# Four adaLN gates: column sums by VectorE and a trip through DRAM instead of an accumulated tile summed by TensorE

## The chip, the core and the metric

The kernel runs on one NeuronCore of a Trainium2 chip, in one launch. The metric is the device time of one execution in microseconds. Weights and activations lie in DRAM at the start; the output goes back to DRAM. The engines named below are TensorE (PE; its weight loads are PEld), VectorE (DVE), ScalarE (ACT), GpSimd (POOL) and SyncE (SP), which here only issues DMAs.

## The reference, cut to what matters

```python
def reference(x, c, ada_w, ada_b, na_w_qkv, na_rpb, na_w_o, fn_w_o, ...):
    cs = jax.nn.silu(c)
    for i in range(DEPTH):                               # DEPTH = 2, D_MODEL = 1024, SEQ = 512
        mod = jnp.einsum('bd,de->be', cs, ada_w[i]) + ada_b[i]
        sh1, sc1, g1, sh2, sc2, g2 = jnp.split(mod[:, None, :], 6, axis=-1)
        u = x * (1.0 + sc1) + sh1
        y = neighborhood_attention(u, ...) if i % 2 == 0 else fourier_mix(u, ...)
        x = layer_norm(ALPHA * x + (1.0 + g1) * y, ln1_g[i], ln1_b[i])
        u = x * (1.0 + sc2) + sh2
        y = conv_ffn(u, ...)                             # D_FF = 2816
        x = layer_norm(ALPHA * x + (1.0 + g2) * y, ln2_g[i], ln2_b[i])
    return x
```

Everything is float32. The four gates `g1`, `g2` of the two layers are vectors of 1024, each the product of the vector `cs` with a 1024x1024 block of `ada_w`, plus a bias. `1 + g` multiplies a sub-layer's output along the channel axis.

## The kernel before, in words

Each float32 matmul is done as three products of values split into a high and a low part (`mm3`), 128 rows by up to 512 columns each. Weights come in tiles of 512 KB into four `raw` buffers; ScalarE writes the high part (line 228), VectorE the low part (line 229). TensorE then works through these stages: the first q, k and v products; neighbourhood attention over eight pairs of heads; the output product `wo`; the first FFN's `up` (22 tiles `f`) and `dn` products; the Fourier mixer; the second FFN.

The conditioning weights, 12 blocks of 1024x1024, come in pieces `ada_l_v_k` through the same four `raw` buffers between the other weights, so that their loads and VectorE's work on them lie beside the matmuls. Blocks that are needed as a column per partition (shifts and scales) lie transposed in DRAM, and VectorE multiplies each piece with `cs_row` and sums it into one column (`weigh_rows`, line 128). The four gates, v = 2 and v = 5 of each layer, are needed as a row on all partitions, since channels lie along the free axis there. For them VectorE accumulates `acc += piece * cs[k]` over eight pieces (lines 151 and 153). `gate_row` then loads the bias row to all partitions (line 176), splits `acc` into a high and a low part in two halves (lines 166 and 167), sums it over the partitions by four products with a matrix of ones into two PSUM banks, and adds 1 and the bias row (line 185). This happens at pair i = 0 of the attention for the first gate, at f = 8 of the first `up`, f = 1 of the first `dn` and f = 14 of the second `up` for the others.

What sets the order: a tile scheduler places the instructions of each engine by its own estimate of times and by the buffers that are free; every engine, SyncE's DMA queue among them, then runs its list in that order, and a waiting instruction holds those behind it. Parts of the program are kept in written order on some engines (the first products, and the attention's pairs from i = 1). Buffers are shared by tags: four `raw`, two `bx` (slices of the position bias, for one head each, from which GpSimd builds the tiles `bm`, lines 514 to 520), six PSUM banks `bank` and two `aux`, thirty `big` tiles of 4 KB per partition.

The stretch around the first gate goes as follows. TensorE makes the value products of the second half of the heads (`v`, four banks), transposes the probabilities of heads 0 and 1 (`pt`), multiplies the scores of the next pair (`s`), the values (`av`), and then the q and k of pair 2 (`qk`). There are six banks. `v` holds four, the first head's `pt` the other two; the second head's `pt` takes the banks of the first two `v` once VectorE has moved these out, and `av` takes those of the second head's `pt`, once VectorE has written their low parts `ptl`. VectorE can do that when ScalarE has written the high parts `pth`.

Of the kernel before, what the change touches and what calls it, by code (L numbers as in the profile page):

```python
# [10 lines left out]
F32 = mybir.dt.float32  # L11
F32R = mybir.dt.float32r
AF = mybir.ActivationFunctionType
ALU = mybir.AluOpType

P = 128
# [38 lines left out]
def tile_hybrid_encoder(ctx: ExitStack, tc: tile.TileContext, xT, x, cols_d, rows_d, ada0, ada_w, wqk0, wqk, wv,  # L55
# [24 lines left out]
    def f32(ap):  # L80
        return ap.bitcast(F32)
# [11 lines left out]
    nc.sync.dma_start(out=cols, in_=cols_d)  # L93
    ident = const.tile([P, P], F32, name="ident")
    make_identity(nc, ident)
    ones_r = const.tile([P, P], F32R, name="ones_r")
    G.memset(f32(ones_r), 1.0)
    mhalf = const.tile([P, 1], F32, name="mhalf")
    G.memset(mhalf, -0.5)

# [22 lines left out]
            A.copy(out=cs_row[:, h * 512 : (h + 1) * 512], in_=b[h])  # L123


    def weigh_rows(raw, c, col, start):

        return V.tensor_tensor_reduce(out=raw, in0=raw, in1=cs_row[:, c], op0=ALU.mult, op1=ALU.add, scale=1.0,  # L128
                                      scalar=start, accum_out=col)

    def ada_columns(l, v, result):

        for k in range(KT):
            raw = wraw.tile([P, D], F32, tag="raw", name=f"ada_{l}_{v}_{k}")
            nc.sync.dma_start(out=raw, in_=ada_w[ADA[(l, v)], k])
            if k == 0:
                col = const.tile([P, KT], F32, name=f"col_{l}_{v}")
            weigh_rows(raw, slice(0, D), col[:, k : k + 1], adab(l, v)[:, k : k + 1])
            if k == KT - 1:
                result[(l, v)] = col  # L140
            yield

    def ada_accumulate(l, v, result):

        acc = None
        for k in range(KT):
            raw = wraw.tile([P, D], F32, tag="raw", name=f"ada_{l}_{v}_{k}")
            nc.sync.dma_start(out=raw, in_=ada_w[ADA[(l, v)], k])
            if k == 0:
                acc = bigt([P, D], F32, f"acc_{l}_{v}")  # L150
                V.tensor_scalar(out=acc, in0=raw, scalar1=cs[:, 0:1], scalar2=None, op0=ALU.mult)
            else:
                V.scalar_tensor_tensor(out=acc, in0=raw, scalar=cs[:, k : k + 1], in1=acc, op0=ALU.mult,
                                       op1=ALU.add)
            if k == KT - 1:
                result[(l, v)] = acc
            yield

    def ada_row_sums(acc, name):

        res = []
        for h in range(2):
            a = acc[:, h * 512 : (h + 1) * 512]
            hi = tmp.tile([P, 512], F32R, tag="t", name=f"{name}_hi{h}")
            lo = tmp.tile([P, 512], F32R, tag="t", name=f"{name}_lo{h}")
            A.copy(out=hi, in_=a)
            V.tensor_tensor(out=lo, in0=a, in1=f32(hi), op=ALU.subtract)
            b = bank(f"{name}_{h}", aux=True)
            mm(b, ones_r, hi, True, False)
            mm(b, ones_r, lo, False, True)  # L170
            res.append(b)
        return res

    def bcast_row(r, name):
        t = bigt([P, D], F32, name)
        nc.sync.dma_start(out=t, in_=rows_d[r : r + 1, :].to_broadcast([P, D]))
        return t

    def gate_row(accs, l, v, name):

        row = bcast_row(ROW_GATE + 2 * l + (0 if v == 2 else 1), f"{name}_row")
        bs = ada_row_sums(accs[(l, v)], name)
        for h in range(2):
            r = row[:, h * 512 : (h + 1) * 512]
            V.scalar_tensor_tensor(out=r, in0=bs[h], scalar=1.0, in1=r, op0=ALU.add, op1=ALU.add)
        return row

    def modulation(sh, sc, ln, name):

# [176 lines left out]
        return raws  # L366

    done = {}
    ada01 = const.tile([P, KT], F32, name="ada01")
    V.tensor_scalar(out=ada01, in0=adab(0, 1), scalar1=1.0, scalar2=None, op0=ALU.add)  # L370

    def cond(k):

        for b, start in enumerate((adab(0, 0), ada01)):
            o = mod0[:, (1 - b) * KT + k : (1 - b) * KT + k + 1]
            start = start[:, k : k + 1]
            if k == 0:
                half = sml.tile([P, 1], F32, tag="t0", name="half")
                weigh_rows(raws[k][b][:, 0:512], slice(0, 512), half, start)
                done["mod"] = weigh_rows(raws[k][b][:, 512:D], slice(512, D), o, half)  # L380
            else:
                done["mod"] = weigh_rows(raws[k][b], slice(0, D), o, start)
# [235 lines left out]

    def ada_iter():
        for l, v in ADA:  # L620
            yield from (ada_accumulate if v in (2, 5) else ada_columns)(l, v, accs)

    ada = ada_iter()

# [19 lines left out]
    for i in range(PAIRS - 1):  # L644
# [6 lines left out]
            qbank, kbank = proj_qk(i + 1)  # L651
            QK[i + 1] = evict_q(i + 1, qbank), evict_k(i + 1, kbank)
        if i == 0:
            gates[(0, 2)] = gate_row(accs, 0, 2, "g1_0")
        transpose_probs(i)
        if i + 2 == PAIRS:
            W.emit(iwo[3])
# [157 lines left out]
    def steps_up0(f):  # L815
        if 2 < f < 19:
            ada_step(2)
        if f == 8:
            gates[(0, 5)] = gate_row(accs, 0, 5, "g2_0")
        if f == FT - 1:  # L820
            W.emit(idn[0][0] + 1)
        if f == 16:
# [21 lines left out]
    def steps_dn0(f):  # L844
        if f < 8:
            ada_step(2)
        if f == 1:
            gates[(1, 2)] = gate_row(accs, 1, 2, "g1_1")
        if f == 8:
            fst["m3"] = modulation(accs[(1, 3)], accs[(1, 4)], (1, 0), "ffn1")  # L850
        if f == 8:
# [111 lines left out]
    def steps_up1(f):  # L963
        if f > 2:
            ada_step(1)
        if f == 14:
            gates[(1, 5)] = gate_row(accs, 1, 5, "g2_1")
        if f == FT - 1:
            W.emit(idn[1][0] + 1)

# [26 lines left out]
def _layouts(inputs):  # L997
# [30 lines left out]

    def piece(l, v):
        w = f["ada_w"][l][:, v * D : (v + 1) * D]  # L1030
        return (w if v in (2, 5) else w.T).reshape(KT, P, D)

    r["ada0"] = np.ascontiguousarray(np.stack([piece(0, 0), piece(0, 1)], axis=2))
    r["ada_w"] = np.ascontiguousarray(np.stack([piece(l, v) for l, v in ADA]))
# [59 lines left out]
```

## Time and profile before

| What | us |
| --- | --- |
| median of three runs | 1049.3 |
| lowest and highest run | 1049.18, 1050.73 |
| the profiled execution | 1050.14 |
| its span | 1048.1 |
| TensorE busy in the span | 1029.5 (98%) |
| VectorE, ScalarE, GpSimd busy | 759.5, 425.2, 102.6 |

The profiled execution lies 0.84 us above the median, and 2.0 us of it lie outside the span. A TensorE row of 128x512 is busy for 0.37 to 0.40 us, but the next one starts after 0.23 us: the rows overlap. So the work of TensorE is counted by starts, not by busy time, and a busy share near 100% hides short pauses. A row of a DMA queue shows the issue alone, not the transfer; rows that follow each other are merged, and their time then includes the waits between them. In brackets stands the idle time before a row and what ended it.

### The profile page before, as it was taken

Reading aid. Unit: us, or ns where it says so; the run is one execution under the profiler, and the core shown is the slowest. Engines: PE = TensorE matmul, PEld = TensorE weight load, DVE = VectorE, ACT = ScalarE, POOL = GpSimd, SP = SyncE. Lnnn points to the kernel's source line nnn. Section 1 sums busy time; section 2 is a strip of 40 time slices with the busy share of each in tenths; the row PEclk is TensorE's granted clock in tenths of the full one; section 3 lists DMA queues with packets and bytes.
Section 4 is the critical chain, followed back from the end, with each engine's and each line's share of the span. In section 5 each row is a group of like instructions: output and inputs, shape, how many; then the busy total and the mean of one; then the engine's idle time right before and its main releaser. Section 6 shows DMA issues by size and latency. Waiting matters only on the chain.

```text
span 1048.1 us, 13339 instructions
## 1 busy us (share of the span) xinstructions
PE 1029.5 (98%) x5032; PEld 862.9 (82%) x5032; DVE 759.5 (72%) x1218; ACT 425.2 (41%) x720; POOL 102.6 (10%) x136
## 2 busy tenths in 40 slices
PE   6999999999999999999999999999999999999996
PEld 5888888889888888888888888898888888888885
DVE  6888999786899888866654788968876566532366
ACT  3536656546444344443232054363444434422200
POOL 0244575500000000000000000000000000000000
PEclk9999999999999999999999999999999999999999
DMA  9985363630455665644884005123443332343301
GB/s 349 330 294 188 115 193 119 219 121 4 145 176 187 217 216 181 201 141 132 280 278 159 1 26 188 69 81 124 142 156 121 121 100 81 90 151 112 110 21 60
DMA packets 46288, 157.21 MB, mean 150 GB/s; under 512 B 5136, under 2 KB 7696, under 8 KB 46224
## 3 DMA queue, kind: packets, MB, share of 16 engines
q1 hardware_dynamic: 46080, 156.24, 45.0%
q8 instruction: 39, 0.64, 0.3%
q14 instruction: 25, 0.20, 0.1%
q10 hardware_dynamic: 144, 0.13, 0.0%
HBM read 154.25 MB, written 2.10 MB: 149 GB/s over the span
## 4 chain that ended last, share of the span: by engine, by line
PE 88%; DVE 5%; POOL 2%; DMA 2%; ACT 1%; issue 1%; SPq 0%; DVEq 0%; POOLq 0%; ACTq 0%
PE up L84 44%; PE dn L84 23%; PE qk L84 4%; PE fo L84 4%; PE wo L84 3%; POOL p L566 2%; PE v L84 2%; PE q L84 1%; PE fy L84 1%; PE av L601 1%; DVE p L552 1%; DMA ada<-in_ada_w_dram 1%; PE pt L587 1%; PE s L84 1%; DVE ada L128 1%
## 5 line engine op out<-in xcount | busy, mean ns | idle before, releaser
L229 DVE TENSOR_TENSOR lo<-raw,hi 128x1024 fp32r<-128x1024 f32 (+1 forms) x173 | 209.7, 1221 | 117.0 <-ACT hi L228 116.3
L228 ACT CAST hi<-raw 128x1024 fp32r<-128x1024 f32 (+1 forms) x173 | 179.0, 1044 | 233.5 <-PE up L84 118.8
L84 PE MATMUL dn<-hi,h 128*128 128x512 f32 (+1 forms) x720 | 218.2, 385 | 0.0
L84 PEld LDWEIGHTS dn<-hi,h 128*128 128x128 f32 x720 | 134.2, 188 | 26.9
L84 PE MATMUL up<-u1h,hi 128*128 128x512 f32 (+1 forms) x384 | 142.9, 372 | 0.0
L84 PE MATMUL up<-u3h,hi 128*128 128x512 f32 (+1 forms) x384 | 142.9, 372 | 0.0
L84 PE MATMUL up<-u3h,lo 128*128 128x512 f32 (+1 forms) x384 | 142.7, 372 | 0.0
L84 PE MATMUL up<-u3l,hi 128*128 128x512 f32 (+1 forms) x384 | 142.7, 372 | 0.0
L84 PE MATMUL up<-u1h,lo 128*128 128x512 f32 (+1 forms) x384 | 142.7, 372 | 0.0
L84 PE MATMUL up<-u1l,hi 128*128 128x512 f32 (+1 forms) x384 | 142.7, 372 | 0.0
L84 PE MATMUL dn<-lo,h 128*128 128x512 f32 (+1 forms) x360 | 138.5, 385 | 0.0
L263 POOL TENSOR_TENSOR y<-ve,mhalf 128x1 f32<-128x1 f32 x16 | 10.9, 683 | 826.8 <-DVE ve L261 826.8
L128 DVE CUSTOM_DVE_ANT_0 ada<-ada,cs_row,cols 128x1024 f32<-128x1024 f32 (+1 forms) x56 | 73.4, 1320 | 14.6 <-DMA ada<-in_ada_w_dram 11.7
L84 PEld LDWEIGHTS up<-u1h,hi 128*128 128x128 f32 x384 | 72.4, 188 | 12.6
L84 PEld LDWEIGHTS up<-u3h,hi 128*128 128x128 f32 x384 | 72.4, 188 | 12.6
L84 PEld LDWEIGHTS up<-u1l,hi 128*128 128x128 f32 x384 | 72.4, 188 | 12.5
L84 PEld LDWEIGHTS up<-u3l,hi 128*128 128x128 f32 x384 | 72.4, 188 | 12.4
L84 PEld LDWEIGHTS up<-u3h,lo 128*128 128x128 f32 x384 | 72.4, 188 | 12.4
L84 PEld LDWEIGHTS up<-u1h,lo 128*128 128x128 f32 x384 | 72.4, 188 | 12.3
L84 PEld LDWEIGHTS dn<-lo,h 128*128 128x128 f32 x360 | 67.7, 188 | 13.4
L566 POOL TENSOR_SCALAR p<-p,rs 128x256 f32<-128x256 f32 x64 | 59.8, 953 | 54.5 <-DVE rs L564 54.4
L712 ACT ACTIVATE gel<-conv 128x512 f32<-128x512 f32 x44 | 27.7, 631 | 66.3 <-DVE conv L709 66.0
(195 smaller groups left out, 1561.3 us busy)
## 6 DMA issues: line engine op xcount, KB each, us to landing
raw<-in_up_dram SPq DMA_DIRECT2D x88, 512.0 KB
ada<-in_ada_w_dram SPq DMA_DIRECT2D x80, 512.0 KB
raw<-in_down_dram SPq DMA_DIRECT2D x44, 512.0 KB
ada<-in_ada_dram SPq DMA_DIRECT2D x14, 512.0 KB
raw<-in_wqk_dram SPq DMA_DIRECT2D x13, 512.0 KB
raw<-in_wv_dram SPq DMA_DIRECT2D x8, 512.0 KB
raw<-in_wo_dram SPq DMA_DIRECT2D x8, 512.0 KB
raw<-in_fnwo_dram SPq DMA_DIRECT2D x8, 512.0 KB
```

Of the source, the lines that this page charges most:

```text
L84: return T.matmul(o, lhsT=lhsT, rhs=rhs, start=start, stop=stop)
L128: return V.tensor_tensor_reduce(out=raw, in0=raw, in1=cs_row[:, c], op0=ALU.mult, op1=ALU.add, scale=1.0, scalar=start, accum_out=col)
L228: A.copy(out=hi, in_=raw)
L229: eng.tensor_tensor(out=lo, in0=raw, in1=f32(hi), op=ALU.subtract)
L263: power = G.tensor_tensor(out=y, in0=ve, in1=mhalf, op=ALU.pow)
L552: V.tensor_tensor_reduce(out=pt[hh][:, j, :], in0=banks[half][hh][:, jj * 256 : (jj + 1) * 256], in1=bm[hh][:, min(j, 1), :], op0=ALU.add, ...
L566: norm = G.tensor_scalar(out=pt[:, j, :], in0=pt[:, j, :], scalar1=rs[:, j : j + 1], scalar2=0.0, op0=ALU.mult, op1=ALU.add)
L587: T.transpose(out=o, in_=pt[:, j, f : f + P], identity=ident)
L601: T.matmul(b[:, o : o + e - a], lhsT=v, rhs=z[:, a:e][:, ::-1], start=n == 0 and m == 0, stop=n == 3 and m == 1, skip_group_check=True)
L712: A.activation(out=q, in_=t, func=AF.Square)
```

## The change

All twelve blocks of `ada_w` now lie transposed in DRAM, and VectorE sums the gates' pieces into columns like those of the other blocks, with the bias plus 1 (`ab1`) as the start value. `gate_store` writes the 128x8 column tile to a 1024-vector in DRAM, element by element (`gate_d`), and `gate_load`, some steps later, loads that vector to all partitions. The accumulating function, the row sums with their eight ScalarE copies, VectorE's subtractions and additions, 16 matmuls and the bias row's four loads are gone. The number and size of the loads of `ada_w` are the same.

```diff
-    ones_r = const.tile([P, P], F32R, name="ones_r")
-    G.memset(f32(ones_r), 1.0)
...
+    gate_d = ctx.enter_context(tc.tile_pool(name="dram", bufs=1, space=bass.MemoryType.DRAM)).tile(
+        [DEPTH, 2, D], F32, name="gate_d")
+    ab1 = const.tile([P, DEPTH * 6 * KT], F32, name="ab1")
+    bias0 = adab
+
+    def bias1(l, v):
+        return ab1[:, (l * 6 + v) * KT : (l * 6 + v + 1) * KT]
...
-            weigh_rows(raw, slice(0, D), col[:, k : k + 1], adab(l, v)[:, k : k + 1])
+            weigh_rows(raw, slice(0, D), col[:, k : k + 1], (bias1 if v in (2, 5) else bias0)(l, v)[:, k : k + 1])
...
-    def ada_accumulate(l, v, result):
...
-    def ada_row_sums(acc, name):
...
-    def gate_row(accs, l, v, name):
...
+    def gate_store(l, v):
+
+        nc.sync.dma_start(out=gate_d[l, v // 5].rearrange("(k p) -> p k", p=P), in_=accs[(l, v)])
+
+    def gate_load(l, v):
+
+        t = bigt([P, D], F32, f"gate_{l}_{v}")
+        nc.sync.dma_start(out=t, in_=gate_d[l, v // 5 : v // 5 + 1, :].to_broadcast([P, D]))
+        gates[(l, v)] = t
...
-    ada01 = const.tile([P, KT], F32, name="ada01")
-    V.tensor_scalar(out=ada01, in0=adab(0, 1), scalar1=1.0, scalar2=None, op0=ALU.add)
+    V.tensor_scalar(out=ab1, in0=cols[:, COL_ADAB:COL_LNG], scalar1=1.0, scalar2=None, op0=ALU.add)
...
-            yield from (ada_accumulate if v in (2, 5) else ada_columns)(l, v, accs)
+            yield from ada_columns(l, v, accs)
...
         if i == 0:
-            gates[(0, 2)] = gate_row(accs, 0, 2, "g1_0")
+            gate_store(0, 2)
+        if i == 1:
+            gate_load(0, 2)
...
         if f == 8:
-            gates[(0, 5)] = gate_row(accs, 0, 5, "g2_0")
+            gate_store(0, 5)
+        if f == 11:
+            gate_load(0, 5)
...
         if f == 1:
-            gates[(1, 2)] = gate_row(accs, 1, 2, "g1_1")
+            gate_store(1, 2)
+        if f == 4:
+            gate_load(1, 2)
...
-        if f == 14:
-            gates[(1, 5)] = gate_row(accs, 1, 5, "g2_1")
+        if f == 13:
+            gate_store(1, 5)
+        if f == 16:
+            gate_load(1, 5)
...
-        return (w if v in (2, 5) else w.T).reshape(KT, P, D)
+        return w.T.reshape(KT, P, D)
```

The change moves instructions. In the queue of SyncE, around the weights of the first gate (`ada_2_k`; `ada_4_k` are those of the next block, `raw` from `wqk` the q and k weights of pairs 2 and 3, `bx` the position bias of head 4 in the rows shown), there stood before:

```order
L148 DMA ada_2_3_611<-in_ada_w_dram 128x1024
L148 DMA ada_2_4_614<-in_ada_w_dram 128x1024
L148 DMA ada_2_5_617<-in_ada_w_dram 128x1024
L148 DMA ada_2_6_620<-in_ada_w_dram 128x1024
L148 DMA ada_2_7_623<-in_ada_w_dram 128x1024
L135 DMA ada_4_0_626<-in_ada_w_dram 128x1024
L135 DMA ada_4_1_630<-in_ada_w_dram 128x1024
L213 DMA raw_633<-in_wqk_dram 128x1024
L213 DMA raw_639<-in_wqk_dram 128x1024
L213 DMA raw_902<-in_wqk_dram 128x1024
L213 DMA raw_918<-in_wqk_dram 128x1024
L514 DMA bx_1012<-in_rpb_dram 64x1x264
```

and there stands now:

```order
L141 DMA ada_2_3_612<-in_ada_w_dram 128x1024
L489 DMA bx_998<-in_rpb_dram 64x1x264
L141 DMA ada_2_4_615<-in_ada_w_dram 128x1024
L141 DMA ada_2_5_618<-in_ada_w_dram 128x1024
L141 DMA ada_2_6_621<-in_ada_w_dram 128x1024
L141 DMA ada_2_7_624<-in_ada_w_dram 128x1024
L141 DMA ada_4_0_627<-in_ada_w_dram 128x1024
L141 DMA ada_4_1_631<-in_ada_w_dram 128x1024
L189 DMA raw_634<-in_wqk_dram 128x1024
L189 DMA raw_640<-in_wqk_dram 128x1024
L156 DMA gate_d<-col_2_604 128x8x1
L189 DMA raw_886<-in_wqk_dram 128x1024
```

The first half of head 4's position bias (`bx_998`; each head's comes in two DMAs) has moved up, in front of five more loads of the gate's and the next block's weights; it waits for a `bx` buffer, and so for GpSimd's `bm` of head 2. The store stands between the second and the third load of `wqk`.

On ScalarE, in the same stretch (`hi` from `raw` are the high parts of the `wqk` weights, `v` the value products, `pth` the transposed probabilities), there stood before:

```order
L228 CAST hi_635<-raw_633 128x1024
L443 CAST v_0_749<-v_0_649 128x4x2x64
L228 CAST hi_641<-raw_639 128x1024
L443 CAST v_1_752<-v_1_650 128x4x2x64
L443 CAST v_2_755<-v_2_651 128x4x2x64
L443 CAST v_3_758<-v_3_652 128x4x2x64
L228 CAST hi_904<-raw_902 128x1024
L443 CAST pth_442<-pt_0_779 128x448
L443 CAST pth_442<-pt_1_780 128x448
L228 CAST hi_920<-raw_918 128x1024
L443 CAST pth_444<-pt_0_793 128x448
L443 CAST pth_444<-pt_1_794 128x448
```

and there stands now:

```order
L204 CAST hi_636<-raw_634 128x1024
L418 CAST v_0_750<-v_0_650 128x4x2x64
L418 CAST v_1_753<-v_1_651 128x4x2x64
L204 CAST hi_642<-raw_640 128x1024
L418 CAST v_2_756<-v_2_652 128x4x2x64
L418 CAST v_3_759<-v_3_653 128x4x2x64
L418 CAST pth_443<-pt_0_763 128x448
L418 CAST pth_443<-pt_1_764 128x448
L204 CAST hi_888<-raw_886 128x1024
L204 CAST hi_904<-raw_902 128x1024
L418 CAST pth_445<-pt_0_777 128x448
L418 CAST pth_445<-pt_1_778 128x448
```

Both high parts of pair 3's weights now stand before the second head's `pth`; before, the second of them and one head's `pth` stood in turn. On TensorE, six `qk` products now stand between `pt` and `s`, where before two stood between `s` and `av`, and the four products with ones are gone.

## Rows read from the trace of the kernel before

**Rows 1.** Busy time of each engine over the whole span, from the page.

```profile
PE 1029.5 (98%) x5032; PEld 862.9 (82%) x5032; DVE 759.5 (72%) x1218; ACT 425.2 (41%) x720; POOL 102.6 (10%) x136
```

**Rows 2.** Stretches of the span: length, busy per engine, clock, DMA share, GB/s.

```profile
20.00:52.00 32.00, 32.00 (x140) 26.13 (x140) 27.83 (x40) 17.46 (x24) 6.61 (x6) 1.00 0.94 345
...
64.00:92.00 28.00, 27.48 (x150) 22.61 (x149) 25.50 (x43) 10.64 (x17) 12.56 (x14) 1.00 0.83 277
...
345.00:486.00 141.00, 141.00 (x623) 116.82 (x622) 108.38 (x144) 57.53 (x78) 0.00 (x0) 1.00 0.51 168
```

**Rows 3.** Chain that ended last, 60 to 112 us: start, us, what.

```profile
66.06 3.90 DMA ada<-in_ada_w_dram
...
81.41 5.88 DMA g_row<-in_rows_dram
...
87.31 0.59 DVE g_row L185
87.92 0.29 DVE g_row L185
...
88.52 0.63 DVE ptl L444
...
89.19 2.11 PE av L601 x16
```

**Rows 4.** TensorE in time, 82 to 92 us: start, us, tile, idle before.

```profile
82.67 0.39 PE L84 MATMUL g<-g_hi,ones_r 128*128 128x512 f32 x1
...
83.59 1.99 PE L587 MATMUL pt<-ident,p 128*128 128x128 f32 x16
...
89.19 0.36 PE L601 MATMUL av<-pth,v 128*128 128x192 f32 x1 [0.33 <-DVE ptl L444]
```

**Rows 5.** TensorE in time, 343 to 345 us, beside the second gate.

```profile
343.27 0.39 PE L84 MATMUL up<-u1h,hi 128*128 128x512 f32 x1
343.73 0.50 PE L84 MATMUL g<-g_lo,ones_r 128*128 128x512 f32 x1
```

**Rows 6.** The accumulator tile: count, ns min/median/max, first and last start.

```profile
L153 DVE SCALAR_TENSOR_TENSOR acc<-ada,cs,acc x28: 1276/1281/1551, 64.7 to 791.7; 128x1024 f32<-128x1024 f32 x28
...
L167 DVE TENSOR_TENSOR g_lo<-acc,g_hi x8: 683/688/693, 78.4 to 835.8; 128x512 fp32r<-128x512 f32 x8
L151 DVE TENSOR_SCALAR acc<-ada,cs x4: 725/746/748, 63.4 to 718.0; 128x1024 f32<-128x1024 f32 x4
```

**Rows 7.** GpSimd in time, 61 to 73 us.

```profile
61.65 7.20 POOL L566 TENSOR_SCALAR p<-p,rs 128x256 f32<-128x256 f32 x8 [10.85 <-DVE rs L564]
68.82 1.70 POOL L516 TENSOR_TENSOR bm<-bx,mask 128x256 f32<-128x256 f32 x1
70.48 1.85 POOL L520 TENSOR_TENSOR bm<-bx,mask 128x128 f32<-128x128 f32 x2
```

**Rows 8.** SyncE's queue in time, at 80 us.

```profile
80.73 0.64 SPq L514 DMA_DIRECT2D bx<-in_rpb_dram  x1
```

**Rows 9.** ScalarE in time, 80 to 88 us.

```profile
80.22 1.05 ACT L228 CAST hi<-raw 128x1024 fp32r<-128x1024 f32 x1 [2.19 <-DMA raw<-in_wqk_dram]
...
86.83 1.01 ACT L443 CAST pth<-pt 128x448 fp32r<-128x448 f32 x2
```

**Rows 10.** VectorE in time, 77 to 83 us.

```profile
77.23 1.28 DVE L128 CUSTOM_DVE_ANT_0 ada<-ada,cs_row,cols 128x1024 f32<-128x1024 f32 x1 [0.37 <-DMA ada<-in_ada_w_dram]
...
81.31 1.22 DVE L229 TENSOR_TENSOR lo<-raw,hi 128x1024 fp32r<-128x1024 f32 x1 [0.38 <-ACT hi L228]
82.45 0.68 DVE L444 TENSOR_TENSOR v<-v,v 128x512 fp32r<-128x512 f32 x1
```

**Rows 11.** DMA queue, kind: packets, MB, share of 16 engines.

```profile
q10 hardware_dynamic: 144, 0.13, 0.0%
```

**Rows 12.** TensorE in time, at the start of the span.

```profile
11.72 0.80 PE L84 MATMUL q<-u0h,hi 128*128 128x512 f32 x1 [3.78 <-ACT u0h L392]
...
15.30 0.51 PE L84 MATMUL q<-u0l,hi 128*128 128x512 f32 x1
```

More of the change, by code (lines that the diff above doesn't have):

```diff
@@ L141, in ada_columns @@
             yield
-    def ada_accumulate(l, v, result):
[L145 to L157, printed above, removed]
-    def ada_row_sums(acc, name):
[L161 to L172, printed above, removed]
     def bcast_row(r, name):
@@ L177, in bcast_row @@
         return t
-    def gate_row(accs, l, v, name):
[L181 to L186, printed above, removed]
+    def gate_store(l, v):
[4 more added lines that the diff above has]
+        gates[(l, v)] = t
     def modulation(sh, sc, ln, name):
@@ L368, in tile_hybrid_encoder @@
     done = {}
-    ada01 = const.tile([P, KT], F32, name="ada01")
-    V.tensor_scalar(out=ada01, in0=adab(0, 1), scalar1=1.0, scalar2=None, op0=ALU.add)
+    V.tensor_scalar(out=ab1, in0=cols[:, COL_ADAB:COL_LNG], scalar1=1.0, scalar2=None, op0=ALU.add)
     def cond(k):
-        for b, start in enumerate((adab(0, 0), ada01)):
+        for b, start in enumerate((adab(0, 0), bias1(0, 1))):
             o = mod0[:, (1 - b) * KT + k : (1 - b) * KT + k + 1]
```

## The prediction

> **What bounds the kernel now.** I read the page first: TensorE is busy for 98% of the span [rows 1], and that number hides pauses, since its rows overlap. So I take its pace from a stretch in which it waits for nothing: 623 products in 141.0 us, 0.226 us each [rows 2]. There, in the FFNs, time falls only if TensorE gets fewer products, and VectorE, ScalarE and the DMAs have slack (VectorE 108 of 141 us, DMA share 0.51).
>
> One stretch is different: 64 to 92 us, where the first gate's weights come in. The DMA engines are 0.83 busy there [rows 2], and the chain of waits leaves TensorE: it runs from a load of the first gate's weights issued at 66.06, through the load of the bias row (issued 81.41, 5.88 us), through VectorE's two additions at 87.31 and 87.92, then the `ptl` behind them at 88.52, into TensorE's `av` at 89.19 [rows 3]. TensorE in time says the same: the four products with ones begin at 82.67, `pt` at 83.59, and `av` at 89.19 has waited for `ptl` [rows 4]. In this stretch an earlier or later `av` moves the end by as much, since TensorE has hardly a pause afterwards that could take it up.
>
> **Products removed.** Sixteen 128x512 products with ones go, four per gate. For the three later gates, inside stretches bound by TensorE: 12 x 0.226 = 2.7 us. Beside the second gate the pace is broken: 343.27 to 343.73 is 0.46 us for one product [rows 5], 0.2 more than the pace, as the `g_lo` product waits; that goes too. I count 2.9 us. The four of the first gate belong to the sum of that stretch.
>
> **VectorE and ScalarE.** Before, 28 accumulations of 1.28, 4 of 0.75 and 8 subtractions of 0.69 us: 35.9 + 3.0 + 5.5 = 44.4 us [rows 6], and eight additions of the bias row besides. Now 32 column sums at the 1.28 us that the same operation takes on another block [rows 10]: 41.0 us, and 32 short reads of the accumulator. So VectorE has a few us less to do, ScalarE eight casts less. In the FFNs both lie beside the matmuls: worth nothing. If that cover were gone, it would be a gain, at most the additions' and subtractions' 10 us. The `ab1` addition at the start is 96 columns wide in place of 8, beside ScalarE's exponential: nothing, at most 0.1 us.
>
> **DMAs.** The weights' loads are the same in number and size; the four bias row loads become four gate loads of the same shape. New are four stores of 1024 single elements. For the three later gates, the store stands where the next load would wait for the same weighing, and the gate load comes long before its use; the 0.51 DMA share beside them has room. I take zero for them; a store or load that held SyncE for some us would eat into weights that are split ahead of use by more than one `f`, so 0 to 1 us.
>
> **The first gate's stretch.** Here the order of SyncE's queue decides. The first half of head 4's bias slice now stands in front of `ada_2_4`. There are two `bx` buffers, so it waits until GpSimd has read head 2's, and `ada_2_4` to `ada_2_7`, `ada_4_0`, `ada_4_1` and four q and k weight tiles stand behind it. In the trace GpSimd works on probabilities from 61.65 to 68.85, then on head 2's `bm` until 70.48 + 1.85 = 72.3 [rows 7]. The earliest is 70.5, if the last two pieces took next to no time. VectorE runs out of weights while SyncE waits, and GpSimd's last pieces may be quicker beside an idle VectorE: I take 71.6. The `bx` issue takes 0.64 [rows 8], so `ada_2_4` goes out at 72.3, where it went out at 66.06: 6.2 us late.
>
> It lands 3.9 us after its issue [rows 3], at 76.2. The first q weight tile is six loads later; at 345 GB/s, the rate of the busiest stretch [rows 2], 512 KB take 1.52 us, so it lands at 76.2 + 9.1 = 85.3. Before, ScalarE got it at 80.22 [rows 9]. The queue has caught up a little, and the lag is 5.1 us. All that follows is queued in order: VectorE's low part of that tile (81.31 before) stands in front of the moves of `v` out of PSUM (82.45 before) [rows 10], whose banks the second head's `pt` needs, and ScalarE's second `pth` stands behind the casts of the weights. The same twelve ScalarE instructions lie between the first cast and the second head's `pth` as before, and they took 86.83 - 80.22 = 6.6 us [rows 9]: so `pth` starts at 91.9. Half of it (0.5) and one `ptl` (0.6, [rows 3]) later, `av` starts at 93.0 or 93.1, against 89.19: 3.9 us late. The bias row's additions, which stood before `ptl`, are already out of this.
>
> The store stands between the second and third of the four weight tiles. The fourth lands 4.6 us after the first, at 89.9, and ScalarE wants it at 90.9, so the store may take 1.0 us for nothing. Its cost is not in the trace. From below: 4 KB, nothing. From above: a queue whose 144 packets carry 0.9 KB each shows 0.0%, that is under 0.05% of 16 x 1048.1 us, or 58 ns a packet [rows 11]; 1024 elements over 16 engines are 64 each, at most 3.7 us. I take the middle, 1.9, so 0.9 us of delay: the rows near it are of larger packets and bound it, none is close. `av` is then 4.8 us late.
>
> [...] With 3.7 us the sum would be 1.8 us higher.
>
> On TensorE four more `qk` products now lie ahead of `av`, so four fewer behind it: 4 x 0.226 = 0.9. The stretch ends 4.8 - 0.9 = 3.9 us later than before (bounds: -2.0, if the loads are not late at all, `av` 1.1 earlier as the additions are gone; +6.4 with GpSimd at 72.3 and the store at 3.7).
>
> **Sum.** 1050.14 (the profiled execution) + 3.9 - 2.9 = 1051.1. That execution lies 0.84 us above the median of 1049.3, so I forecast 1050.3. A measurement of this kernel can tell about 0.2% from no change, 2.1 us; the forecast is within it.
>
> **Rivals.** (a) The late loads do no harm: GpSimd frees the buffer early, or the DMA engines, idle for some us, catch up more. For it speaks that four buffers are free when SyncE goes on, so that four loads start at once; against it, that the stretch's DMA share is already 0.83. Then the stretch gives -2.0, the rest -2.9: 1049.3 - 4.9 = 1044.4. Any stretch below +0.8 makes the kernel faster by over 0.2%.
>
> (b) The store is dear. SyncE's `bx` issue of 64 rows took 0.64 us [rows 8], while I gave the store 1.9 in all; if its issue grew with its 1024 elements, SyncE would be held for 10 us in front of the last two q and k tiles. Behind it stand ScalarE's casts, `pth`, `ptl` and `av`. Every us beyond the 1.0 that is free moves the end by one; from about 3.0 us it makes the kernel slower by over 0.2%; at 10 us the store costs 9.0 instead of 0.9, 1058.4. Against it: the DMA issues in the trace differ little in time.
>
> [...]
>
> **How the numbers follow.** Forecast (stretch between +0.8 and +5.0, store under 3 us) 0.48; rival (a) and smaller gains of its kind 0.24; (b) 0.14, (c) 0.14, of which half is slower by over 0.2% by itself or with a late GpSimd, and half stays within. So faster 0.24, within 0.2% 0.55, slower 0.21. Two in ten outside: the low end leaves out the full gain of (a), 1045.0; the high end holds (c) and the upper bound of the store, 1050.3 + 1.8 + 0.7 (GpSimd at 72.3), and a little of (b): 1053.5. The forecast's own range is 1047.2 to 1051.4.
>
> **What would show it.** In SyncE's queue, a gap between `ada_2_3` and `ada_2_4` until GpSimd's third `bm` piece ends, 5 to 7 us; the DMA engines idle within it; the first `wqk` cast about 5 us later than 80.22; `av` near 94; from there to the end a lead of 2.9 us won back. If `ada_2_4` goes out before 69, the main step is wrong; if `av` comes before 90, rival (a); if the cast of the fourth tile waits for its load after the others are done, rival (b); if products at 0.4 us pace follow, rival (c). If the FFN stretches are not shorter by the removed products, the second term is wrong.

## The result and the profile after

| Kernel | median us | runs | of before beside it | ratio (95% interval) |
| --- | --- | --- | --- | --- |
| changed | 1060.51 (1059.75 to 1061.2) | 4 | 1050.01 | 1.0097 (1.0085 to 1.0109) |

The change makes the kernel 10.5 us slower. The forecast was 1050.3 with a range from 1045.0 to 1053.5, so the result lies above it. The profiled execution took 1060.48 us, its span 1058.7.

From the page of the changed kernel, the busy line and the lines on DMA packets:

```profile
PE 1029.9 (97%) x5016; PEld 863.8 (82%) x5016; DVE 753.5 (71%) x1234; ACT 421.8 (40%) x712; POOL 101.6 (10%) x135
...
DMA packets 50448, 157.23 MB, mean 149 GB/s; under 512 B 9296, under 2 KB 11856, under 8 KB 50384
...
q1 hardware_dynamic: 50240, 156.25, 46.4%
```

TensorE has sixteen products fewer than in [rows 1] and VectorE 6.0 us less work, as forecast. Before, queue q1 had 46,080 packets, of which (with the other queues) 5136 were under 512 B; the four stores add 4160, 1040 each: one per element, and 16 more.

The loss lies in the stretch of the first gate. TensorE in time, changed kernel (start, us, tile, idle before):

```profile
83.07 1.03 PE L562 MATMUL pt<-ident,p 128*128 128x128 f32 x8
89.87 1.94 PE L562 MATMUL pt<-ident,p 128*128 128x128 f32 x8 [5.77 <-DVE v L419]
...
92.04 0.63 PE L84 MATMUL qk<-u0l,hi 128*128 128x512 f32 x1
92.47 0.63 PE L84 MATMUL qk<-u0h,lo 128*128 128x512 f32 x1
...
100.64 0.53 PE L576 MATMUL av<-pth,v 128*128 128x192 f32 x1 [4.08 <-DVE ptl L419]
...
114.40 1.91 PE L562 MATMUL pt<-ident,p 128*128 128x128 f32 x16
```

Two pauses, of 5.77 and 4.08 us, stand where [rows 4] had one of 0.33, and `av` starts at 100.64 instead of 89.19. The last row is the end of the stretch, the transposes of pair 1. They stood here before:

```profile
101.73 1.91 PE L587 MATMUL pt<-ident,p 128*128 128x128 f32 x16
```

The stretch ends 12.7 us later; the span as a whole is 10.6 longer, so 2.1 us come back behind it. What delays `av` is read from the chain of waits (start, us, what):

```profile
72.27 0.64 SPq L489
...
73.03 0.36 SPq L141
...
73.50 5.07 DMA ada<-in_ada_w_dram
...
86.26 12.11 DMA raw<-in_wqk_dram
...
98.45 1.04 ACT hi L204
99.49 0.44 ACT pth L418
...
99.96 0.64 DVE ptl L419
...
100.64 3.78 PE av L576 x16
```

The chain holds both steps of the forecast. SyncE issues `bx` at 72.27 and `ada_2_4` at 73.03 (forecast 72.3). Six loads of weights stand behind this `bx` in the queue, as the prediction's sum has it, not five as said in the part ahead of it. But the load of the last `wqk` tile, issued at 86.26, needs 12.11 us, where the first of those six, of the same size, needs 5.07; ScalarE's cast, its second `pth`, VectorE's `ptl` and `av` follow it one after the other. ScalarE and SyncE in time, around the store:

```profile
86.83 1.04 ACT L204 CAST hi<-raw 128x1024 fp32r<-128x1024 f32 x1 [21.68 <-DMA raw<-in_wqk_dram]
...
90.12 1.04 ACT L204 CAST hi<-raw 128x1024 fp32r<-128x1024 f32 x1 [1.28 <-DMA raw<-in_wqk_dram]
...
95.61 1.05 ACT L204 CAST hi<-raw 128x1024 fp32r<-128x1024 f32 x1 [2.60 <-DMA raw<-in_wqk_dram]
98.45 1.04 ACT L204 CAST hi<-raw 128x1024 fp32r<-128x1024 f32 x1 [1.79 <-DMA raw<-in_wqk_dram]
```

```profile
73.03 7.32 SPq L141 DMA_DIRECT2D ada<-in_ada_w_dram  x6
81.42 1.55 SPq L189 DMA_DIRECT2D raw<-in_wqk_dram  x2
83.02 0.43 SPq L156 DMA_DIRECT2D gate_d<-col  x1
84.26 2.33 SPq L189 DMA_DIRECT2D raw<-in_wqk_dram  x2
```

The store's issue holds SyncE for 0.43 us only. The two tiles issued behind it come late, and so does the second tile, issued just ahead of it: its cast waits 1.28 us for it. The stretches say why (columns as in [rows 2]), first in the changed kernel:

```profile
83.00:89.00 6.00, 1.10 (x10) 0.80 (x7) 3.62 (x5) 2.02 (x3) 0.00 (x0) 0.94 1.25 282
89.00:95.00 6.00, 5.13 (x18) 4.12 (x20) 4.81 (x8) 2.89 (x5) 0.00 (x0) 0.50 0.83 80
95.00:101.00 6.00, 1.92 (x25) 1.71 (x23) 1.04 (x2) 2.96 (x4) 1.54 (x3) 0.78 0.72 235
```

then in the kernel before:

```profile
89.00:95.00 6.00, 5.81 (x33) 5.09 (x34) 5.91 (x24) 3.51 (x11) 1.92 (x4) 1.00 0.51 187
```

From 89 to 95 us the DMA engines show the same share, 0.83, as in the second stretch of [rows 2], but move 80 GB/s where they moved 277 there. (The share adds up the times of the packets, and where it lies above 1, as with 1.25 from 83 to 89 us, packets of one engine overlap.) And the granted clock is 0.50 there, while it was 1.00 in this stretch before.

The second pause costs TensorE time of its own behind `av`. The `qk` products that follow start 0.43 us apart at first, not 0.23, and the granted clock from 101 to 107 us is 0.64:

```profile
104.22 0.63 PE L84 MATMUL qk<-u0h,hi 128*128 128x512 f32 x1
104.65 0.63 PE L84 MATMUL qk<-u0l,hi 128*128 128x512 f32 x1
```

### The profile page after: what moved, and what is told of

Same layout as the page of the kernel before. It is cut to its first block, busy times and chain, and to the rows that moved or that the text cites. A ratio compares the mean times of both kernels' runs of the same rounds, so it can differ in the third digit from the quotient of the medians.

```text
span 1058.7 us, 13293 instructions
## 1 busy us (share of the span) xinstructions
PE 1029.9 (97%) x5016; PEld 863.8 (82%) x5016; DVE 753.5 (71%) x1234; ACT 421.8 (40%) x712; POOL 101.6 (10%) x135
## 4 chain that ended last, share of the span: by engine, by line
PE 88%; DVE 4%; DMA 3%; POOL 3%; issue 1%; ACT 1%; SPq 0%; DVEq 0%; POOLq 0%; ACTq 0%
PE up L84 45%; PE dn L84 22%; PE fo L84 4%; PE qk L84 4%; PE wo L84 3%; POOL p L541 2%; PE v L84 2%; DMA ada<-in_ada_w_dram 1%; PE av L576 1%; PE q L84 1%; DMA raw<-in_wqk_dram 1%; PE fy L84 1%; PE pt L562 1%; PE s L84 1%; DVE p L527 1%; PE tr L279 1%
## 5 line engine op out<-in xcount | busy, mean ns | idle before, releaser
L84 PEld LDWEIGHTS up<-u3h,hi 128*128 128x128 f32 x384 | 72.3, 188 | 12.6
L84 PEld LDWEIGHTS up<-u1h,hi 128*128 128x128 f32 x384 | 72.3, 188 | 12.6
L84 PEld LDWEIGHTS up<-u1l,hi 128*128 128x128 f32 x384 | 72.3, 188 | 12.5
L84 PEld LDWEIGHTS up<-u3l,hi 128*128 128x128 f32 x384 | 72.3, 188 | 12.5
L84 PEld LDWEIGHTS up<-u3h,lo 128*128 128x128 f32 x384 | 72.3, 188 | 12.4
L84 PEld LDWEIGHTS up<-u1h,lo 128*128 128x128 f32 x384 | 72.3, 188 | 12.4
```

The source lines that it names most:

```text
L84: return T.matmul(o, lhsT=lhsT, rhs=rhs, start=start, stop=stop)
```

## The experiments

Theory: the single elements of the store occupy the DMA engines, and the wait for the `bx` buffer adds to it. Rivals: the wait alone; any store in this place; the pause and the clock. The table has the medians, each with its ratio to the kernel before on the same chip, and a measure of how late the last `wqk` tiles come: the time from ScalarE's cast of the first to that of the fourth. Where no cast waits for its load, three casts and the six other ScalarE instructions among them take 5.6 us (where third and fourth are one row, the fourth starts 0.95 us after it).

| Run | median us | ratio (95% interval) | first to fourth cast |
| --- | --- | --- | --- |
| changed kernel | 1060.51 | 1.0097 (1.0085 to 1.0109) | 11.6 |
| e1 store in rows of 32 bytes | 1052.98 | 1.0030 (1.0019 to 1.0041) | 5.6 |
| e2 elementwise store, later | 1054.13 | 1.0039 (1.0025 to 1.0053) | 5.6 |
| e3 four `bx` buffers | 1054.74 | 1.0041 (1.0026 to 1.0056) | 12.7 |
| e4 rows and four buffers | 1046.04 | 0.9962 (0.9947 to 0.9977) | 5.6 |
| e5 two elementwise stores | 1067.08 | 1.0162 (1.0145 to 1.0179) | 18.6 |
| e6 512 pieces of 8 bytes | 1053.47 | 1.0029 (1.0017 to 1.0041) | 7.6 |
| e7 rows, and 1024 elements loaded | 1052.86 | 1.0029 (1.0018 to 1.0041) | 5.6 |
| e8 before, four `bx` buffers | 1050.51 | 1.0002 (0.9992 to 1.0011) | |
| e9 rows, and elements 512 bytes apart | 1053.09 | 1.0028 (1.0016 to 1.0040) | 5.6 |
| e10 rows, and elements SBUF to SBUF | 1053.73 | 1.0031 (1.0018 to 1.0044) | 5.6 |
| e11 stores by ScalarE's queue | 1059.27 | 1.0086 (1.0071 to 1.0101) | 12.6 |
| e12 e4, later gates elementwise | 1046.26 | 0.9962 (0.9948 to 0.9976) | 5.6 |
| e13 rows, and neighbours from one partition | 1062.28 | 1.0108 (1.0092 to 1.0123) | 14.3 |
| e14 rows, and the pause filled | 1056.53 | 1.0059 (1.0042 to 1.0076) | 5.6 |
| e15 rows, and elements 64 bytes apart | 1053.23 | 1.0027 (1.0017 to 1.0037) | 5.6 |
| e16 rows, and elements 16 bytes apart | 1052.45 | 1.0021 (1.0010 to 1.0032) | 6.2 |

### Store and buffer, each alone and both (e1 to e4, e8)

e1 permutes a gate's channels (weights and bias columns alike):

```diff
-        nc.sync.dma_start(out=gate_d[l, v // 5].rearrange("(k p) -> p k", p=P), in_=accs[(l, v)])
+        nc.sync.dma_start(out=gate_d[l, v // 5].rearrange("(p k) -> p k", k=KT), in_=accs[(l, v)])
```

> The gates' channels are permuted in the layout of ada_w and of the bias columns (channel p*8+k in partition p, column k), so that the store writes 8 neighbouring elements per partition: 128 pieces of 32 bytes instead of 1024 of 4 bytes. Everything else, the order of SyncE's queue too, is as in the changed kernel. Theory (the 1024 single elements hold up the loads queued behind the store): the store lands some 3 us after its issue instead of 12.1, the fourth wqk tile is cast near 91 instead of 98.45, av starts near 94 to 95 instead of 100.64, the time is 1051 to 1054. Rival A (the wait for the bx buffer, so the late weights, is the whole loss): fourth cast, av and the time stay as in the changed kernel, 1060. Rival B (any store in this place makes the loads behind it wait, whatever its pieces): the same, 1060. Rival C (the pause of TensorE and the clock after it are the larger part): av still late by the pause, 1056 or more.

e2 moves store and load of the first gate from pairs 0 and 1 to pairs 2 and 3:

```diff
-        if i == 0:
+        if i == 2:
             gate_store(0, 2)
-        if i == 1:
+        if i == 3:
             gate_load(0, 2)
```

> Same elementwise store, but the first gate's store and load stand at pairs 2 and 3 instead of 0 and 1, behind the loads of wqk for pairs 2 and 3 (and the first of pair 4) in SyncE's queue. The order of the queue ahead of that is unchanged. Theory: the fourth wqk tile is cast near 91 and av starts near 94 to 95, as with the store in rows; the store then delays by some 10 us the loads behind it at its new place (bx and wqk of pair 4), which may cost part of it again: 1051 to 1056. Rival A (the bx wait alone): 1060, av near 100. Rival B (the loss comes with any store there): 1051 to 1054, as the theory, so that this run alone does not tell them apart.

e3 has four buffers, e4 this and the store in rows, e8 four buffers in the kernel before:

```diff
-        bx = tmp.tile([P, NBIAS], F32, tag="bx", name=f"bx{head}", bufs=2)
+        bx = tmp.tile([P, NBIAS], F32, tag="bx", name=f"bx{head}", bufs=4)
```

> Four bx buffers instead of two, nothing else: the slices of head 4 need no buffer that GpSimd still reads, so SyncE does not wait in front of ada_2_4. Theory (wait and store add up): ada_2_4 goes out near 66 instead of 73.03, the first wqk tile is cast near 80 to 81 instead of 86.83; the store still takes 12 us to land and the fourth tile comes 6 us earlier than 98.45, near 92; av near 94 to 95, time 1054 to 1055. Rival A (the bx wait is the whole loss): av near 88, time 1047 to 1048. Rival D (the store alone is the loss, and the wait is hidden by it): time stays at 1059 to 1061.

> Both: the store in rows of 32 bytes and four bx buffers. Theory: the first gate's stretch is as long as before or up to 2 us shorter, the FFN stretches are 2.9 us shorter by the removed products (2.1 were seen in the changed kernel's trace): 1045 to 1048, faster than before by 0.2 to 0.5%. If column sums by VectorE themselves cost time in that stretch, over 1050.

> The kernel before with four bx buffers, nothing else. A control: in the kernel before no load of weights stood behind the wait for a bx buffer, so the buffers alone should be worth nothing, 1049 to 1051. If they are worth more, that much of the gain of the version with both edits is theirs and not the change's.

All five times lie where the theory had them (e2 and e1 differ by less than their intervals). e1 rules out that the wait alone, or any store in this place, is the whole loss: both gave 1060. Against the kernel before beside them, the changed kernel stands at +10.5 us, e1 at +2.9, e3 at +4.7, e4 at -4.0. So the store's pieces cost 7.6, the wait 5.8, and the two together 14.5. Each is worth more once the other is gone (8.7 and 6.9), but that difference of 1.1 us is within the intervals. e8 shows that the buffers alone are worth nothing. e4 beats both kernels. In e1 (VectorE, then TensorE):

```profile
93.16 1.16 DVE L419 TENSOR_TENSOR ptl<-pt,pth 128x448 fp32r<-128x448 f32 x2 [0.27 <-ACT pth L418]
```

```profile
89.05 1.94 PE L562 MATMUL pt<-ident,p 128*128 128x128 f32 x8 [5.57 <-DVE v L419]
...
91.22 0.63 PE L84 MATMUL qk<-u0l,hi 128*128 128x512 f32 x1
91.64 0.63 PE L84 MATMUL qk<-u0h,lo 128*128 128x512 f32 x1
...
95.47 0.36 PE L576 MATMUL av<-pth,v 128*128 128x192 f32 x1
...
107.07 1.91 PE L562 MATMUL pt<-ident,p 128*128 128x128 f32 x16
```

The first `ptl` is done at 93.7 (half of 1.16 after 93.16); `av` starts at 95.47 without a pause before it: TensorE itself is late, since its `qk` products start 0.42 us apart after the pause instead of 0.226. The stretch ends 5.3 us later than before (107.07 against 101.73). In e4 that pause is gone:

```profile
84.30 0.63 PE L562 MATMUL pt<-ident,p 128*128 128x128 f32 x4 [0.82 <-DVE v L419]
...
89.10 0.36 PE L576 MATMUL av<-pth,v 128*128 128x192 f32 x1
...
100.71 1.91 PE L562 MATMUL pt<-ident,p 128*128 128x128 f32 x16
```

The same work of TensorE, from the second head's `pt` to `av`, takes 4.80 us here (84.30 to 89.10, at a granted clock of 1.00) and 6.42 in e1 (89.05 to 95.47). The stretch ends 1.0 us earlier than before, and the span (1044.2) is 3.9 shorter: the other 2.9 us come behind it, as much as was forecast for the products removed later.

### What of the store costs (e5 to e7, e9 to e11)

e5 repeats the elementwise store of the first gate in the changed kernel, to another vector laid out alike:

```diff
         nc.sync.dma_start(out=gate_d[l, v // 5].rearrange("(k p) -> p k", p=P), in_=accs[(l, v)])
+        if (l, v) == (0, 2):
+            nc.sync.dma_start(out=gate_2, in_=accs[(l, v)])
```

> The changed kernel with a second elementwise store of the first gate's column, to another 1024-vector that nothing reads, right behind the first in SyncE's queue. Theory (the elements occupy the queue that the loads behind them use, some 7.5 us per store by the difference of the changed kernel and the one with the store in rows): the fourth wqk tile is cast near 106 instead of 98.45, av near 108, time 1067 to 1070. Rival (the store has a long latency and the loads behind it wait for its end, but two stores run side by side): 1060 to 1062.

e6 writes pairs of channels, with weights and bias permuted to match:

```diff
-        nc.sync.dma_start(out=gate_d[l, v // 5].rearrange("(k p) -> p k", p=P), in_=accs[(l, v)])
+        nc.sync.dma_start(out=gate_d[l, v // 5].rearrange("(k p t) -> p k t", p=P, t=2), in_=accs[(l, v)].rearrange("p (k t) -> p k t", t=2))
```

> The gates' channels are permuted so that the store writes 512 pieces of 8 bytes (two neighbouring channels per partition and piece). Theory (cost goes with the number of pieces): about half of the 7.5 us between 1024 pieces and 128: 1055.5 to 1057.5, the store lands some 8 to 9 us after its issue. Rival (each piece that is not as long as a row of 32 bytes costs more than its number, or the cost is a fixed one): 1060.

e11 issues the four stores of the changed kernel from ScalarE:

```diff
-        nc.sync.dma_start(out=gate_d[l, v // 5].rearrange("(k p) -> p k", p=P), in_=accs[(l, v)])
+        nc.scalar.dma_start(out=gate_d[l, v // 5].rearrange("(k p) -> p k", p=P), in_=accs[(l, v)])
```

> The changed kernel with its four elementwise stores issued by ScalarE's DMA queue instead of SyncE's; ScalarE's issue stands in front of its cast of the first wqk tile. Theory (the 16 DMA engines are busy with the elements, and every queue shares them): the two last wqk tiles still land some 4 to 8 us late, the time is 1056 to 1061. Rival (the loads wait only because they are queued behind the store on the same queue): they land as with the store in rows, near 89 and 91, and the time is 1052.5 to 1054.5.

The second store costs another 6.3 us (16.8 over the kernel before beside it, instead of 10.5). For e6 the time forecast was a miss: 1053.47, as e1. The delay itself is there, and about a third of the changed kernel's. ScalarE's cast of the fourth tile waits for its load:

```profile
93.67 1.05 ACT L204 CAST hi<-raw 128x1024 fp32r<-128x1024 f32 x1 [1.07 <-DMA raw<-in_wqk_dram]
```

This cast comes 2.0 us later behind the first than in e1, and that is nearly free, because TensorE, at a granted clock of 0.60 from 89 to 95 us, reaches `av` no earlier than 95.47 in e1 anyway; the rows of the chain put it at 95.86 here. That slack was not in my expectation. e11 shows that a queue of its own does not help (9.1 us over the kernel before, the changed kernel 10.5): from 89 to 95 us the DMA engines show a share of 1.00 at 65 GB/s.

```profile
89.00:95.00 6.00, 4.50 (x14) 3.42 (x14) 0.62 (x2) 0.81 (x1) 0.00 (x0) 0.50 1.00 65
```

e11 also tells the store's packets from the loads', since each has its own queue. Queues from 84 to 100 us (packets, MB, share of the 16 engines), first e11's loads (q1) and store (q10), then e1's q1:

```profile
q1 hardware_dynamic: 923, 2.79, 94.9%
q10 hardware_dynamic: 1040, 0.00, 3.7%
```

```profile
q1 hardware_dynamic: 1158, 3.08, 58.5%
```

The store's own packets take 3.7% of 16 us, 0.6 us on each engine. What grows is the time of the other queue's packets: 15.2 us on each engine for 2.79 MB, where 3.08 MB took 9.4 in e1. So the elements do not fill the engines by their own recorded time, as the theory had it; the loads' packets last longer beside them.

e7, e9 and e10 add to e1, right behind the first gate's store, 1024 single elements each: loaded from DRAM, written to DRAM 512 bytes apart, and copied from SBUF to SBUF. Nothing reads any of them. Each adds 1040 packets to q1 (47,696 against 46,656), as many as one elementwise store; so do e13, e15 and e16 below.

```diff
+            nc.sync.dma_start(out=extra, in_=rows_d[ROW_LNG].rearrange("(k p) -> p k", p=P))
```

```diff
+    lines = dram2.tile([D, P], F32, name="lines")[:, 0].rearrange("(k p) -> p k", p=P)
...
+            nc.sync.dma_start(out=lines, in_=accs[(l, v)])
```

```diff
+    extra2 = const.tile([P, 2 * KT], F32, name="extra2")
...
+            nc.sync.dma_start(out=extra2[:, ::2], in_=extra)
```

> The kernel with the store in rows of 32 bytes, and behind the store of the first gate a load of 1024 single elements of a constant vector into a 128x8 tile that nothing reads (VectorE writes the tile first, so that the load stands in the same place of SyncE's queue). Theory (the number of pieces is the cost, in either direction): as the elementwise store, 1059 to 1061. Rival (writing less than a line is the cost, and loads of single elements are cheap): 1053 to 1054.5, as without the load.

> The kernel with the store in rows, and behind the first gate's store a second one of 1024 single elements, each to its own 512 bytes of DRAM (the column of a 1024x128 array that nothing reads). Theory (the cost is that of each small write to DRAM, wherever it goes): the fourth wqk tile lands some 8 us later than the 90.63 of the kernel in rows, the time is 1059 to 1061. Rival (128 elements share each 512 bytes, and writes to the same piece of memory wait for each other): the tile lands within 2 us of 90.63, the time is 1053 to 1054.

> The kernel with the store in rows, and behind the first gate's store a copy of 1024 single elements from SBUF to SBUF (a 128x8 tile into every second column of a 128x16 tile that nothing reads), by the same queue. Theory (the write to DRAM is what costs): no delay, as with the load of single elements, the fourth wqk tile lands within 1 us of 90.63, 1052.5 to 1054.5. Rival (reading 4 bytes at a time from SBUF is what costs): the tile lands some 8 us later, 1059 to 1061.

In e7 and e9 the theory as I had it fell: neither the number of pieces nor the small write as such is dear (1052.86 and 1053.09, where e1 has 1052.98). ScalarE's third and fourth casts run through without a wait, first in e7, then in e9:

```profile
90.19 2.04 ACT L208 CAST hi<-raw 128x1024 fp32r<-128x1024 f32 x2
```

```profile
91.53 2.04 ACT L208 CAST hi<-raw 128x1024 fp32r<-128x1024 f32 x2
```

### How close the elements lie (e13, e15, e16)

e13 writes 1024 single elements into 4 KB with neighbours from one partition; e15 and e16 are e9 with arrays of [1024, 16] and [1024, 4] instead of [1024, 128].

```diff
+    lines = dram2.tile([D], F32, name="lines").rearrange("(p k) -> p k", k=KT)
...
+            V.tensor_scalar(out=wide[:, ::2], in0=accs[(l, v)], scalar1=1.0, scalar2=None, op0=ALU.mult)
+            nc.sync.dma_start(out=lines, in_=wide[:, ::2])
```

> The kernel with the store in rows, and behind the first gate's store a second one of 1024 single elements into 4 KB of DRAM that nothing reads, its source a 128x16 tile of which every second column is taken, its target packed with channel p*8+k: neighbouring elements in DRAM come from one partition and follow each other in the list, whereas the changed kernel's neighbours come from neighbouring partitions. Theory (sharing 512 bytes is enough): the fourth wqk tile lands some 8 us later than the 90.63 of the kernel in rows, time 1059 to 1061. Rival (only elements written at the same time by different DMA engines to one place wait for each other): it lands within 3 us, time 1053 to 1054.5.

> As the run with each element in its own 512 bytes, but the elements 64 bytes apart (a column of a 1024x16 array): 8 elements in each 512 bytes, 64 KB in all. The reading is the cast of the fourth wqk tile, 91.6 in the kernel with the store in rows, near 100 where 1024 packed elements are written. Theory (every write waits for those before it in the same 512 bytes, so the delay goes with the elements per 512 bytes, 8 of 128): under 1.5 us later than 91.6, time 1053 to 1054.5. Rival (any two that share 512 bytes are enough): 97 or later, 1058 to 1062.

> The elements 16 bytes apart: 32 in each 512 bytes, 16 KB in all. Theory (delay by elements per 512 bytes, 32 of 128): 2 to 3 us later than 91.6 for the fourth tile, most of it inside the 3 us that the run with 512 pairs showed to be free: 1053 to 1055. Rival (any sharing is enough): 97 or later, 1058 to 1062. Rival (only elements that share less than 16 bytes wait, or the cost is that of a smaller unit): no delay, 1053.

Packed into 4 KB the elements are dear again, whichever partition the neighbours come from (from the first to the fourth cast 14.3 us in e13 and 11.6 in the changed kernel, 5.6 in e1); 16 bytes apart they are nearly free (6.2 in e16). ScalarE's casts in e13 and e16:

```profile
98.35 1.04 ACT L210 CAST hi<-raw 128x1024 fp32r<-128x1024 f32 x1 [6.86 <-DMA raw<-in_wqk_dram]
100.96 1.04 ACT L210 CAST hi<-raw 128x1024 fp32r<-128x1024 f32 x1 [1.57 <-DMA raw<-in_wqk_dram]
```

```profile
91.14 1.05 ACT L208 CAST hi<-raw 128x1024 fp32r<-128x1024 f32 x1 [0.40 <-DMA raw<-in_wqk_dram]
```

And the stretch from 89 to 95 us in e13, then in e9: the DMA share is high in both, but they move 66 and 271 GB/s.

```profile
89.00:95.00 6.00, 5.27 (x36) 4.62 (x37) 4.58 (x7) 2.49 (x5) 0.00 (x0) 0.72 1.14 66
```

```profile
89.00:95.00 6.00, 5.07 (x18) 4.06 (x20) 6.00 (x10) 5.44 (x9) 1.90 (x2) 0.51 0.87 271
```

### The later gates, and the clock (e12, e14)

e12 is e4 with the three later gates stored element by element; e14 is e1 with 24 products that nothing reads between the two heads' transposes:

```diff
+            if head == 1:
+                fb = bank("fill", aux=True)
+                for n in range(24):
+                    mm(fb, u0[0][n % 4][:, 0, 0:P], u0[0][n % 4][:, 1, :], True, True)
```

> The version with rows and four bx buffers, in which only the three later gates are stored element by element again. Theory: in the FFNs the loads behind such a store land 9 us late, but the weights are split ahead of use by more than that, so it costs nothing: 1045.5 to 1046.7. Rival (each of the three stalls TensorE a little, as 0.41 us beside the third gate's in the changed kernel's trace): 1046.5 to 1048.

> The kernel with the store in rows (bx wait kept), and 24 products of 128x512 that nothing reads between the two heads' transposes of pair 0, where TensorE pauses for 5.6 us: 24 x 0.226 = 5.4 us of work. The scheduler then also puts the six qk products behind av again. Theory (the pause costs twice: once itself, once by the clock behind it, granted 0.60 in 89 to 95 us): the transposes after the pause run at 1.0 clock, the stretch ends 1.5 to 2.2 us earlier, 1050.8 to 1051.5. Rival (the work at the slow clock lay beside waits for VectorE and ScalarE anyway): 1052.5 to 1053.5.

The later stores cost nothing that can be measured (1046.26 beside 1046.04 from another chip). In the changed kernel, the 12 us behind the second gate's store show the same picture, 59 GB/s at a share of 0.76 (before: 170 at 0.47), and a TensorE that is busy throughout:

```profile
345.00:357.00 12.00, 12.00 (x55) 9.93 (x54) 6.71 (x10) 2.21 (x3) 0.00 (x0) 1.00 0.76 59
```

e14 missed, and settles nothing on the clock's price. The filled pause kept the second head's eight transposes fast (1.03 us, in e1 1.94) and the granted clock at 1.00 from 89 to 95 us, but the scheduler put the `qk` products behind `av` and both low parts of weights in front of the second `ptl`, so that TensorE paused later:

```profile
89.81 1.03 PE L566 MATMUL pt<-ident,p 128*128 128x128 f32 x8
...
96.09 0.53 PE L580 MATMUL av<-pth,v 128*128 128x192 f32 x1 [1.83 <-DVE ptl L419]
```

## Why the prediction was wrong

**The step that failed: the store's cost.** The prediction bounded the store by 3.7 us from above and took 1.9, of which 0.9 was to matter. The runs give it 7.6 us. The bound was one on the time of the store's own packets, from a queue whose 144 packets show a share of 0.0% [rows 11]. That time was not set too low: in e11 the 1040 packets take 0.6 us on each engine. What the sum left out, without a reason, is what packed single elements do to the loads beside them, whose packets fill 94.9% of the engines' time there instead of 58.5%. The trace of before holds no such store, so no row of it bounds this. The last cast's delay grows with the packed pieces: 2.0 us for 512 of 8 bytes (e6), 6.0 for 1024 of 4 (the changed kernel), 13.0 for 2048 (e5). e13 shows it when neighbours come from one partition too; e7, e9 and e10 show that elements loaded, spread or kept in SBUF are not dear.

**Rival (b)** had the size (up to 10 us) and the victims (the last two tiles, `pth`, `ptl`, `av`), but the wrong place: SyncE's issue takes 0.43 us, and the loads in the DMA engines are what is held. Its sign, the fourth tile's cast waiting for its load, came true, by another mechanism; that its 1058.4 lies near the 1060.51 is luck. It had a chance of 0.14, with the argument that issues differ little in time; that was true of the issue (0.33 to 0.82 us each in the trace of before, 0.43 for this store) and said nothing of the transfer.

**SyncE's wait for the `bx` buffer** was right: `ada_2_4` at 73.03 (forecast 72.3), the first `wqk` cast at 86.83 (85.3). GpSimd's last two pieces took their full time, 1.85 us from 70.38, with VectorE busy until 71.5 (two more, from 72.89 beside an idle VectorE, took 0.87): the upper bound of [rows 7], which is 0.7 us of this. And the first load behind took 5.07 us instead of the 3.9 of [rows 3]; the loads after it made up 0.4. e3 prices it at 5.8 us, pause and clock included.

**Rival (c), the clock,** has 0.14 of the chances and is held in the high end of the range. No run shows the term that it adds there; what the runs showed in its place comes beside the store. Its sign came true: `qk` products 0.42 us apart in e1 and 0.43 in the changed kernel. After pauses of 5.77 us (changed) and 5.57 us (e1) the clock is granted at 0.50 and 0.60 from 89 to 95 us. In e1 `av` could start at 93.7 by its inputs, near the forecast's 93.0 without the store, and starts at 95.47: 1.7 us; the same work at a granted clock of 1.00 in e4 is 1.6 us shorter. What comes late in e1 is the transposes and six `qk`. Late starts alone do not show the clock: at the start of the span before, nine starts took 3.58 us [rows 12], eight intervals of 0.45 each, with the granted clock recorded as 1.00. In the changed kernel the second pause, of 4.08 us, adds to the loss: from `av` to the transposes of pair 1 TensorE needs 13.76 us (100.64 to 114.40, granted 0.64 from 101 to 107), in e1 11.60 (95.47 to 107.07, granted 1.00 from 95) for the same products. These 2.2 us are part of what the store costs. No run takes the clock's price out by itself.

**The removed products** came out in size, though no run takes them out alone. Between the transposes of pair 1 and the end, e4 gains 2.9 us, as forecast; the changed kernel 2.1. A short pause of TensorE in the first `dn` of the changed kernel, 0.64 us between two starts, is part of the difference; the rest was not traced:

```profile
502.37 0.50 PE L84 MATMUL dn<-hi,h 128*128 128x512 f32 x1 [0.25 <-DVE conv L693]
```

**Relief of VectorE and ScalarE** showed no gain beyond this, and **the three later stores** cost nothing, though the DMA engines moved 59 GB/s behind the second one, 170 before: the cover that the prediction named held.

**The sum.** Forecast for the stretch +3.9, measured +12.7: the store 7.33 (12.67 less the 5.34 of e1; 5.17 of it up to `av`, 2.16 by the clock behind it), the clock behind the first pause 1.7 of the 5.34, and the wait's remaining 3.6, against 3.0 forecast for it with a free store.

## What to carry to other kernels

When a DMA writes a column per partition into a packed row of DRAM, lay out the channels so that each partition writes several neighbours in one piece: here 32 bytes instead of 4 took 7.6 us off, at no other cost. A transfer that the trace does not show has no upper bound there, and its own packets' time need not be its cost (0.6 us on each engine in e11, where the store cost 7.6 in the changed kernel): let the range stay open, or look at what the DMA engines move per busy share once it runs. And read what a moved load waits for: two buffers more took off 5.8 us, and with the store in rows besides, a change that lost 10.5 us gained 4.0.

## What the runs showed of the hardware

The number of single-element pieces alone says little. Packed into 4 KB of DRAM, 1024 elements of 4 bytes hold up the loads behind them by 6.0 us (changed kernel) to 8.7 us (e13), by the casts; 16 bytes apart by 0.6; 64 or 512 bytes apart, loaded from DRAM, or copied within SBUF, by nothing that a cast waits for. So it is writing many neighbours within a few bytes of each other that holds up the loads, while the store's own packets are short (0.6 us on each engine in e11). The size of a write alone does not do it: e9's elements are as small as e13's, and from the first to the fourth cast it took 5.6 us against 14.3. What in the writing of close neighbours holds up the loads was not shown, nor the distance from which on it stops; pairs of 8 bytes, packed, lie between (2.0 us). After pauses of TensorE of 5.77 and 4.08 us the granted clock was 0.50 and 0.64 over the stretches behind them (89 to 95 and 101 to 107 us); with the first pause filled (e14) it stayed at 1.00 there.
